# Clearing the other semaphores under the last store, with one wait that takes the store's semaphore back to zero

## Chip, cores, metric

One core of one Trainium2 chip. The metric is the device time of one execution in microseconds (us), taken as the median of several executions. A *span* is the time from the first to the last instruction of the program in the trace. A *semaphore* is a counter that engines and transfers change and that engines wait for. "Landing" is the last of the sixteen increments by which a transfer reports to its semaphore. A *drain* (DRAIN in the lists) is the instruction with which an engine lets its own work end: in the kernel before, those of ScalarE and VectorE ended 34 and 48 ns behind the last work of their engine. Engines are named as in the views: SP issues the transfers here, DVE is VectorE, ACT ScalarE, POOL (Pool) GpSimd, PE TensorE; a q behind the name (POOLq) marks the engine's sequencer, with its waits, drains and semaphore instructions.

## The reference

```python
batch, seq, dim = 32, 512, 1024
x = np.random.randn(batch, seq, dim).astype(np.float32)      # 67.1 MB
return np.sum(x, axis=-1).astype(np.float32)                 # 16384 sums
```

## The kernel before

The body loads seven tiles of 128 x 16 rows and pieces of an eighth, sums them on VectorE (part of the last ones on ScalarE), and stores 16384 sums with two transfers. The one that ends last is issued by SP:

```python
        hold(store(nc.scalar, 0, last), two, "its packets come behind those of the loads")
        halves(whole[:, :1], part)
        halves(sums[:, j : j + 1], whole)
        store(nc.sync, last, last + 1)          # 8 KB, reports to semaphore 105
```

Behind the body the framework puts an end: all engines meet at a barrier (each reports to a "gather" semaphore, Pool passes it and raises a "release" semaphore), Pool clears the semaphores 99 to 108 that the program used, and all meet again. The kernel rewrites this end. SP no longer waits for the store; Pool's clear does, and Pool passes the second gather ahead of it:

```python
def wait_for_the_store_at_the_clear(nc):
    end = nc.main_func.blocks[-1]
    insts = list(end.instructions)
    ...                                   # take the wait for the last store off SP's drain
    clear = next(k for k, i in enumerate(insts)
                 if i.engine == mybir.EngineType.Pool and isinstance(i, mybir.InstISA))
    insts[clear] = copy.replace(
        insts[clear], sync_info=mybir.SyncInfo(on_wait=[wait], on_update=[])
    )
    at = next(k for k in range(clear + 1, len(insts))
              if insts[k].engine == mybir.EngineType.Pool
              and isinstance(insts[k], mybir.InstEventSemaphore))
    met = insts.pop(at)                   # Pool's side of the second gather
    insts.insert(clear, met)
    end.instructions = insts
```

Pool's last instructions are thus: gather, clear of ten semaphores that waits for 105, drain, release.

## Time and profile before

| | kernel before |
|---|---|
| time, first three runs | 161.58, 161.58, 161.99 us |
| span of the profiled run (161.66 us) | 159.88 us |
| last vector sum ends | 158.10 us |
| last store issued / landed | 158.127 / 159.563 us |
| Pool's last instruction ends / span ends | 159.789 / 159.877 us |

Lines of the page and of the list of the last instructions are in the prediction. One view more is needed later: the chain of work that ended last, in order of time (start us, us, what). Lines from its middle and its end, kernel before:

```profile
66.94 40.78 DMA t<-in_x_dram
107.72 0.02 issue
107.75 17.23 DVE sums L141
...
126.33 31.29 DMA t<-in_x_dram
157.62 0.07 issue
157.69 0.40 DVE t L155
158.09 0.01 DVEq L253
```

A line "DMA" is the wait for one load, from issue to landing. Such waits take up most of the chain, and it stops with the last sum at 158.1 us. What follows is no work to the profile, yet it takes 1.78 us to the end of the span. All numbers below that are finer than the views print are the trace's own time stamps.

### The profile page before, as it was taken

The numbers are of one execution on the slowest core, as the hardware profiler recorded it, in microseconds if no ns is written. First come the engines' busy times: TensorE is split into PE (matmuls) and PEld (weight loads), VectorE is DVE, ScalarE is ACT, GpSimd is POOL, SyncE is SP. The second block draws the span as 40 slices with busy tenths as digits, with TensorE's granted clock in tenths as the row PEclk, the third lists the DMA queues.
The fourth block names the chain that finished last, engine by engine and source line by source line (L and its number), as shares of the span: only waits on it lengthen the run. The fifth ranks groups of instructions, "written<-read, shape, count | busy, mean of one in ns | idle before, by whom it ended". The sixth has DMA issues, their size and how long they took to land.

```text
span 159.9 us, 132 instructions
## 1 busy us (share of the span) xinstructions
DVE 120.6 (75%) x40; ACT 12.0 (8%) x21; POOL 0.2 (0%) x4
## 2 busy tenths in 40 slices
DVE  0029600499985999779995899949999499994955
ACT  3000000000000000000000000000000000003993
POOL 0000000000000000000000000000000000000000
DMA  8899899799699699699699699799898996996994
GB/s 308 380 492 525 361 426 525 328 459 525 295 492 525 262 525 525 262 525 525 262 525 508 279 525 476 312 525 410 377 525 361 426 525 262 525 525 289 400 384 124
DMA packets 2784, 67.18 MB, mean 420 GB/s; under 512 B 1248, under 2 KB 1376, under 8 KB 1504
## 3 DMA queue, kind: packets, MB, share of 16 engines
q1 hardware_dynamic: 1872, 67.12, 97.7%
q10 hardware_dynamic: 912, 0.06, 0.4%
HBM read 67.11 MB, written 0.07 MB: 420 GB/s over the span
## 4 chain that ended last, share of the span: by engine, by line
DMA 71%; DVE 27%; SPq 1%; issue 0%; DVEq 0%
DMA t<-in_x_dram 71%; DVE sums L141 26%; SPq L180 0%; SPq L222 0%; DVE t L155 0%; DVEq L253 0%
## 5 line engine op out<-in xcount | busy, mean ns | idle before, releaser
L141 DVE TENSOR_REDUCE sums<-t 128x16 f32<-128x16384 f32 (+1 forms) x7 | 110.9, 15848 | 33.4 <-DMA t<-in_x_dram 33.4
L168 ACT ACTIVATE unread<-t 128x1024 f32<-128x1024 f32 x10 | 10.1, 1013 | 144.7 <-DMA t<-in_x_dram 144.7
L155 DVE CUSTOM_DVE_ANT_0 t<-t 128x512 f32<-128x512 f32 (+2 forms) x16 | 9.6, 654 | 4.1 <-DMA t<-in_x_dram 4.0
L168 ACT ACTIVATION_READ_ACCUMULATOR unread<-t 128x1 f32 x10 | 1.9, 188 | 0.0
L168 ACT ACT_TABLE_LOAD x1 | 1.3, 1283 | 0.8 <-PEq L242 0.8
L155 DVE DVE_READ_ACCUMULATOR2_ANT sums<- 128x1 f32 x15 | 1.2, 81 | 0.0
L242 POOL MEMSET const-bfloat16-1.0<- 128x1 bf16 x1 | 0.1, 102 | 0.0
L242 POOL MEMSET const-uint8-127<- 128x1 uint8 x1 | 0.1, 102 | 0.0
L242 POOL MEMSET const-float32-1.0<- 128x1 f32 x1 | 0.1, 99 | 0.0
L242 POOL MEMSET const-float32-0.0<- 128x1 f32 x1 | 0.1, 98 | 0.2 <-issue 0.2
L155 DVE DVE_READ_ACCUMULATOR2_ANT t<- 128x1 f32 x1 | 0.1, 83 | 0.0
L220 DVE MEMSET t<- 128x1 f32 x1 | 0.1, 59 | 0.0
## 6 DMA issues: line engine op xcount, KB each, us to landing
t<-in_x_dram SPq DMA_DIRECT2D x1, 3584.0 KB, 11.0
t<-in_x_dram SPq DMA_DIRECT2D x1, 3072.0 KB, 28.9
t<-in_x_dram SPq DMA_DIRECT2D x1, 1024.0 KB, 31.0
t<-in_x_dram SPq DMA_DIRECT2D x1, 280.0 KB, 31.2
t<-in_x_dram SPq DMA_DIRECT2D x1, 232.0 KB, 31.3
t<-in_x_dram SPq DMA_DIRECT2D x7, 40.8
out_dram<-sums ACTq DMA_DIRECT2D x1, 56.0 KB, 2.1
out_dram<-sums SPq DMA_DIRECT2D x1, 8.0 KB, 1.4
```

Of the source, the lines that this page charges most:

```text
L141: return nc.vector.tensor_reduce(out=dst, in_=src, axis=mybir.AxisListType.X, op=mybir.AluOpType.add)
L155: return nc.vector.tensor_tensor_reduce(out=src[:, :n], in0=src[:, :n], in1=src[:, n:], scale=1.0, scalar=0.0, op0=mybir.AluOpType.add, op ...
L168: nc.scalar.activation(out=unread[:, :n], in_=src, func=mybir.ActivationFunctionType.Copy, accum_out=dst,)
L220: nc.vector.memset(whole[:, width + 1 :], 0.0)
L242: nc = _bacc.Bacc("TRN2", target_bir_lowering=False, num_devices=1)
```

## The change

The intent: of the ten semaphores only 105 must wait for the store. So the other nine are cleared while the store is under way, and so is Pool's drain passed. Behind the landing stands one semaphore instruction that waits for 105 and subtracts the value again, then the release.

```diff
-    insts[clear] = copy.replace(
-        insts[clear], sync_info=mybir.SyncInfo(on_wait=[wait], on_update=[])
-    )
 ...
-    met = insts.pop(at)
-    insts.insert(clear, met)
+    both = insts[clear]
+    lo, hi = both.ant_dict["range_first"], both.ant_dict["range_last"]
+    def ranged(first, last):
+        instr = list(both.instr)
+        instr[13:15] = first, last
+        ant_dict = dict(both.ant_dict, range_first=first, range_last=last)
+        return copy.replace(
+            both, name=nc.get_next_instruction_name(), instr=instr, ant_dict=ant_dict
+        )
+    ...                                   # met, drain: Pool's side of the second gather and
+                                          # its drain, which stood behind the clear
+    (gather,) = met.sync_info.on_update
+    back = copy.replace(
+        gather, id=wait.id, ant_name=wait.ant_name, update_value=wait.wait_value
+    )
+    taken = copy.replace(
+        met,
+        name=nc.get_next_instruction_name(),
+        sync_info=mybir.SyncInfo(on_wait=[wait], on_update=[back]),
+    )
+    insts = [i for i in insts if i is not met and i is not drain]
+    insts[clear : clear + 1] = [
+        met,
+        ranged(lo, wait.id - 1),
+        ranged(wait.id + 1, hi),
+        drain,
+        taken,
+    ]
     end.instructions = insts
```

More of the change, by code (lines that the diff above doesn't have):

```diff
@@ L82, in wait_for_the_store_at_the_clear @@
     )
-    info = insts[clear].sync_info
-    assert info is None or not (info.on_wait or info.on_update)
-    insts[clear] = copy.replace(
-        insts[clear], sync_info=mybir.SyncInfo(on_wait=[wait], on_update=[])
-    )
-    at = next(
-        k
-        for k in range(clear + 1, len(insts))
-        if insts[k].engine == mybir.EngineType.Pool and isinstance(insts[k], mybir.InstEventSemaphore)
-    )
-    assert insts[at].sync_info.on_wait and "gather" in insts[at].sync_info.on_wait[0].ant_name
-    met = insts.pop(at)
-    insts.insert(clear, met)
+    both = insts[clear]
+    assert both.op_name == "EVENT_SEMAPHORE_RANGE_CLEAR"
+    assert both.sync_info is None or not (both.sync_info.on_wait or both.sync_info.on_update)
+    lo, hi = both.ant_dict["range_first"], both.ant_dict["range_last"]
+    assert (both.instr[13], both.instr[14]) == (lo, hi) and lo < wait.id < hi
+    def ranged(first, last):
[5 more added lines that the diff above has]
+        )
+    met, drain = [
+        insts[k]
+        for k in range(clear + 1, len(insts))
+        if insts[k].engine == mybir.EngineType.Pool
+        and isinstance(insts[k], (mybir.InstEventSemaphore, mybir.InstDrain))
+    ][:2][::-1]
+    assert isinstance(met, mybir.InstEventSemaphore) and isinstance(drain, mybir.InstDrain)
+    (gather,) = met.sync_info.on_update
+    back = copy.replace(
+        gather, id=wait.id, ant_name=wait.ant_name, update_value=wait.wait_value
+    )
+    taken = copy.replace(
+        met,
+        name=nc.get_next_instruction_name(),
+        sync_info=mybir.SyncInfo(on_wait=[wait], on_update=[back]),
+    )
+    insts = [i for i in insts if i is not met and i is not drain]
[6 more added lines that the diff above has]
+    ]
     end.instructions = insts
```

## The prediction

> **What bounds the kernel now.** I read the page first: the busy shares, the slices and the chain that ended last.
>
> ```profile
> span 159.9 us, 132 instructions
> DVE 120.6 (75%) x40; ACT 12.0 (8%) x21; POOL 0.2 (0%) x4
> DMA  8899899799699699699699699799898996996994
> DMA 71%; DVE 27%; SPq 1%; issue 0%; DVEq 0%
> ```
>
> The first line is the length of the program on the core; the third is the DMA engines' busy share in 40 slices of 4 us. The kernel reads 67.11 MB and its body is a stream of loads with vector sums behind them: loads and sums make up 98% of the chain. The change touches none of it. It concerns what stands after the last sum, where the chain of the page stops (at 158.1 us), because the page counts waits, drains and semaphore instructions as no work. So I went on to the views of the end: the list of line L253 (the end of the program) and the stores.
>
> ```profile
> L253 POOLq EVENT_SEMAPHORE_RANGE_CLEAR  x1: 93/93/93, 159.6 to 159.6; - x1
> L253 POOLq DRAIN  x1: 34/34/34, 159.7 to 159.7; - x1
> L253 POOLq EVENT_SEMAPHORE  x1: 17/17/17, 159.8 to 159.8; - x1
> L253 SPq EVENT_SEMAPHORE  x1: 17/17/17, 159.8 to 159.8; - x1
> L253 ACTq EVENT_SEMAPHORE  x1: 17/17/17, 159.8 to 159.8; - x1
> L253 DVEq EVENT_SEMAPHORE  x1: 21/21/21, 159.8 to 159.8; - x1
> L253 PEldq EVENT_SEMAPHORE  x1: 51/51/51, 159.8 to 159.8; - x1
> ...
> out_dram<-sums SPq DMA_DIRECT2D x1, 8.0 KB, 1.4
> ```
>
> Columns of the first seven: engine, operation, count, shortest/median/longest duration in ns, start in us. They are the last seven instructions, from 159.58 us on; the eighth line is the last store, 8 KB, 1.4 us from issue to landing. The views print starts to a tenth of a us. This change needs nanoseconds, so I read the trace's own time stamps (us from the span's start):
>
> - 158.093: the last vector sum ends; 158.127 to 158.475: SP issues the last store, on semaphore 105.
> - 158.877 to 158.894: Pool passes the first gather barrier; 158.955 to 158.972: it releases the others; 159.036 to 159.106: its drain.
> - 159.180: the fourth engine reports to the second gather; 159.204 to 159.221: Pool passes it. From here Pool stands still for 366 ns.
> - 159.386 to 159.563: the sixteen increments of semaphore 105 arrive, 12 ns apart. The last is the landing of the store.
> - 159.587 to 159.680: range clear of semaphores 99 to 108, which waits for 105 to reach 32. The ten land between 159.608 and 159.652 in bunches of four, four and two, about 20 ns apart.
> - 159.709 to 159.743: Pool's drain. 159.772 to 159.789: Pool releases the other four. 159.814 to 159.877: they leave; PE's 51 ns end the span.
>
> So what bounds the tail is the store's landing, and after it a row of 314 ns (159.877 - 159.563) in series on Pool: 24 to wake, 93 clear, 29 gap, 34 drain, 29 gap, 17 release, and 88 until PE is out.
>
> **What the Trainium skill says.** Perfetto Trace Analysis, section "Sequencer-only Instruction (DRAIN, etc)": the profiler's start is the moment at which all semaphores are satisfied, and neither the wait nor the propagation of an update is in the duration. The trace agrees: durations are 7 to 93 ns, and what costs as much are the gaps (24, 29, 61 ns), so I count start to start. DMA: Bandwidth & Descriptors, section "Why a DMA increments its semaphore by 16 and not by 1": each engine that a store uses adds 1 after its own data, and only the full count means that all has landed. The trace shows exactly sixteen increments of 105, over 177 ns. It follows that 105 must not be cleared before 159.563, while the rest of the range has no such bar. Runtime: NRT & Kernel Launch, section "The ~15µs preamble/postamble breakdown": after the kernel come barriers and a reset of the semaphores. No view here names these stages; the profiled run took 161.66 us against a span of 159.88, so 1.78 us of the metric lie outside the span and the change does not touch them.
>
> **The change, part by part.** Pool's end was: gather, [wait 105] clear 99-108, drain, release. It becomes: gather, clear 99-104, clear 106-108, drain, [wait 105, subtract 32], release. The other four engines and all of the body stay as they are.
>
> What moves ahead of the landing, timed from 159.204 where the gather is passed (unchanged): A semaphore instruction that also updates is followed by the next one 78 ns after its own start: Pool's 158.877 to 158.955, and the same pair at the beginning of the program, 0.582 to 0.660. So the first clear starts at 159.282. The old clear shows 21 ns before its first write, bunches 20 ns apart, and 28 ns after the last write: 93 for three bunches. Six semaphores are two bunches, about 73 ns; three are one, about 51 ns (estimates from this one instruction). With the 29 ns gap seen behind the old clear: first clear 159.282 to 159.355, second 159.384 to 159.435, drain (34) 159.464 to 159.498, ready for the wait at about 159.527. The landing comes at 159.563 and is noticed at 159.587 (24 ns, as the old clear was, and as the gather's 159.180 to 159.204). There are some 60 ns of slack to the noticed landing. If each clear costs a full 93 ns whatever its range, the sum is 159.282 + 93 + 29 + 93 + 29 + 34 + 29 = 159.589, which is late by 2 ns. So this part is free, or nearly, in this trace.
>
> What stays behind the landing: the wait-and-subtract starts at 159.587; the release starts 78 ns later, at 159.665. The pair is of the very form of the two gather/release pairs above, only with another semaphore and 32 in place of 4. Before, the release started at 159.772: 93 + 29 + 34 + 29 = 185 ns after the wake. The gain is 185 - 78 = 107 ns. From the release to the end of PE's exit are 105 ns, unchanged (159.772 to 159.877). The span becomes 159.77.
>
> What it adds: two instructions on Pool (one clear more, and the wait-and-subtract), both counted above. The sum: 161.58 - 0.107 = 161.47 us, or 0.07% less. I choose the median of before as base, which two of the three runs hit.
>
> **The rivals.** First, *the early work isn't hidden after all*: the landing must come after the drain is done. For: the slack is only 60 ns, and the sixteen increments of 105 arrive (159.386 on) just while the clears write to the neighbours of 105. If a clear is held back, or if the gap behind it is 61 ns rather than 29, Pool is late. Against: even with two clears of 93 ns and every gap at 61, the wait starts at 159.282 + 93 + 61 + 93 + 61 + 34 + 61 = 159.685, 98 ns later than the landing is noticed, and the gain is 107 - 98 = 9 ns: 161.57. A dear case costs nothing, it only eats the gain. Second, *the subtraction is dearer than on the barrier's semaphores*, as 105 has just been written to by sixteen DMA engines. The gather's 96 is also written by four engines just before and shows no such cost; I put it at 0 to 50 ns: 161.47 to 161.52. Third, *the end of the span moves and the time doesn't*, because the 1.78 us outside it wait for something else, an instruction fetch for instance. In this trace the next write to a semaphore comes 235 ns after the span's end, and nothing shows what it waits for: 161.58. Fourth, *the runs scatter by more than the gain*: the three runs of before lie 0.41 us apart and the profiled one gives 161.66. That is four times the gain, and it comes from the stream of loads, where one delayed transfer moves all of the rest. For a median from another chip I allow 0.3 us either way.
>
> **Range and chances.** All mechanisms together lie between 161.47 and 161.58, so scatter sets the width: 161.15 to 161.8. For 2% it would take 3.2 us; the whole tail from the last sum to the end of the span is 1.78 us (158.093 to 159.877). Faster by 2% can't come from here, and slower by 2% would need a disturbed run. I give 0.99 to the same, and the rest to accidents.
>
> **What would show it.** In the trace of the changed kernel: two range clears on Pool, both ended before the last increment of 105, the first shorter than 93 ns and the second shorter still; a Pool drain ended before it too; one more Pool semaphore instruction of 17 ns that starts 24 ns after the landing; the release 78 ns behind that; and 207 ns, not 314, from landing to the end of the span. These differences within one trace hold even if the span itself moves by several tenths through its loads. It is wrong if a clear or the drain still stands after the landing, if the step from the wait to the release is much over 78 ns, or if the landing itself comes later after its issue than 1.44 us (158.127 to 159.563), which would mean that the clears disturb it. The time is wrong in its mechanism if landing to end shrinks by 107 ns and interleaved timed runs of both kernels show no difference near 0.1 us; a difference of several tenths either way I would read as the loads' scatter.

## The result and the profile after

The changed kernel: 161.89 us median of six runs (161.45 to 162.05), the kernel before 161.60 us median of six (161.55 to 161.99), ratio 1.0009 with a 95% interval of 0.9993 to 1.0026: the same. A ratio here is the mean time of one kernel's fast runs over that of the other's of the same rounds, so not quite the ratio of the medians. Executions over 1.5% slower than the fastest of the same kernel are left out of the means.

So no gain shows, rather the opposite by 0.09%. The profile of the changed kernel (a run of 161.81 us) has to say which part of it is the change. Its end, as the list of the end's instructions (columns as in the prediction), first the stretch from the gather to the landing, then the one behind the landing:

```profile
L279 POOLq EVENT_SEMAPHORE_RANGE_CLEAR  x2: 46/58/71, 159.6 to 159.7; - x2
L279 POOLq DRAIN  x1: 34/34/34, 159.7 to 159.7; - x1
```

```profile
L279 POOLq EVENT_SEMAPHORE  x2: 17/17/17, 159.9 to 159.9; - x2
L279 SPq EVENT_SEMAPHORE  x1: 17/17/17, 160.0 to 160.0; - x1
L279 ACTq EVENT_SEMAPHORE  x1: 17/17/17, 160.0 to 160.0; - x1
L279 DVEq EVENT_SEMAPHORE  x1: 21/21/21, 160.0 to 160.0; - x1
L279 PEldq EVENT_SEMAPHORE  x1: 51/51/51, 160.0 to 160.0; - x1
```

There are two clears of 71 and 46 ns where one of 93 stood, and they and the drain have left the stretch behind the landing. Only two semaphore instructions of 17 ns and the four exits remain there. The time stamps: gather 159.473, clears 159.554 to 159.625 and 159.651 to 159.697, drain to 159.760, landing 159.827, wait-and-subtract 159.851, release 159.930, end of the span 160.034. From landing to end are 207 ns, before they were 314.

Yet the span is 160.03 us, longer by 0.16. The same chain as above, changed kernel:

```profile
67.05 40.99 DMA t<-in_x_dram
108.04 0.02 issue
108.07 17.23 DVE sums L167
...
126.68 31.22 DMA t<-in_x_dram
157.90 0.06 issue
157.96 0.40 DVE t L181
158.36 0.01 DVEq L279
```

The sums take 17.23 us as before; the load of 40.78 us took 40.99, and the last sum ends at 158.37 us in place of 158.10. So the body came 0.27 us later, and the end is 0.11 us shorter; together 0.16 more. Is the later body chance, or did the change cause it? And does the shorter end reach the time at all? These are the questions for the experiments.

### The profile page after: what moved, and what is told of

It reads as the page before. It is cut to its first block, busy times and chain, and to the rows that moved or that the text cites. A ratio compares the mean times of both kernels' runs of the same rounds, so it can differ in the third digit from the quotient of the medians.

```text
span 160.0 us, 134 instructions
## 1 busy us (share of the span) xinstructions
DVE 120.6 (75%) x40; ACT 11.9 (7%) x21; POOL 0.2 (0%) x4
## 4 chain that ended last, share of the span: by engine, by line
DMA 71%; DVE 27%; SPq 1%; issue 0%; DVEq 0%
DMA t<-in_x_dram 71%; DVE sums L167 26%; SPq L206 0%; SPq L248 0%; DVE t L181 0%; DVEq L279 0%
```

## The experiments

Twelve kernels ran. For each full-size kernel one profile gives a row of this table; all are in us. "Landing to time" is the time of the profiled execution minus its landing, so the body and its scatter are out of it. Tail kinds: see the sections below.

| profile of | last sum ends | landing to Pool's end | landing to span's end | time | time - Pool's end | time - span's end | landing to time |
|---|---|---|---|---|---|---|---|
| before | 158.10 | 0.226 | 0.314 | 161.66 | 1.871 | 1.783 | 2.097 |
| changed | 158.37 | 0.120 | 0.207 | 161.81 | 1.863 | 1.776 | 1.983 |
| e1, changed again | 158.08 | 0.118 | 0.207 | 161.53 | 1.870 | 1.781 | 1.988 |
| e2, before again | 158.76 | 0.226 | 0.314 | 162.31 | 1.866 | 1.778 | 2.092 |
| e3, dear tail | 157.95 | 1.097 | 1.185 | 162.38 | 1.874 | 1.786 | 2.971 |
| e4, wait last | 158.07 | 0.081 | 0.081 | 161.48 | 1.872 | 1.872 | 1.953 |
| e8, shortest end | 158.50 | 0.040 | 0.040 | 161.88 | 1.883 | 1.883 | 1.923 |
| e9, drain alone | 158.39 | 0.162 | 0.250 | 161.88 | 1.871 | 1.783 | 2.033 |
| e10, clears alone | 158.07 | 0.185 | 0.272 | 161.58 | 1.869 | 1.782 | 2.054 |
| e11, ScalarE tail | 158.00 | 0.119 | 0.475 | 161.44 | 1.865 | 1.509 | 1.984 |
| e12, before again | 158.00 | 0.225 | 0.313 | 161.55 | 1.864 | 1.776 | 2.089 |

My theory after the result: the end is 107 ns shorter in every execution, and the loads scatter by several tenths of a us whichever end follows. Rival A: the change disturbs the loads. Rival B: the time outside the span swallows what happens at the span's end. Runs 1 to 4 shared a chip and their runs of the kernel before (161.57 us median of eleven); so did 5 to 8. Of 9 to 11 only the profile was taken.

### e1: the changed kernel again

Edit: a comment.

> The changed kernel, unchanged but for a comment, in more timed runs. My theory (the tail is 107 ns shorter, and the stream of loads scatters by several tenths of a us whichever tail follows): landing of the last store to end of span 207 ns again (205 to 209), the last vector sum ends anywhere from 157.9 to 158.6 us, times from 161.4 to 162.1 us, and a ratio to the kernel before between 0.998 and 1.002. Rival A (the change disturbs the loads, so that they end later): ratio over 1.001 again, and the last sum ends near 158.36 us, as in the first trace of the changed kernel, not near 158.09.

Measured: 161.59 us median of six (161.38 to 162.27), ratio 1.0002 (0.9984 to 1.0021). One run lies above the range that I gave (162.27) and one just below it (161.38). The last sum ends at 158.08 us, earlier than in the first profile of the kernel before; landing to end is 207 ns. Rival A, which had the last sum near 158.36 again, falls in its simple form.

### e2: the kernel before against itself

Edit: a comment in the kernel before.

> The kernel before against itself, the same program under a new name. My theory: here too the times of one kernel lie in two clusters or a band some 0.5 us wide (161.5 to 162.1), and the ratio to itself strays from 1 by up to 0.002, so that 1.0009 of the changed kernel is what no change at all can give. Landing to end of span 314 ns. Rival A: the kernel before stays close to 161.6 us (all but one of six runs did), ratio within 0.0005 of 1.

Measured: 161.89 us median of five (161.68 to 162.31) against 161.57 for the very same program, ratio 1.0012 (0.9997 to 1.0026). Two names of one program differ by more than the changed kernel differed from it. The chain of this run, from the same places as above:

```profile
66.97 41.49 DMA t<-in_x_dram
108.46 0.02 issue
108.48 17.23 DVE sums L141
...
158.35 0.40 DVE t L155
158.75 0.01 DVEq L253
```

The load of 40.78 us took 41.49 here, with nothing changed. The starts of the seven big sums show how it comes: 19.31 to 19.36 us lie between one and the next in the first profile of the kernel before; here three of the six steps are 19.67, 19.65 and 19.45; in the first profile of the changed kernel 19.49, 19.42 and 19.38 stand out. A few tiles come late, now these, now those, and little of it is made up: the seventh big sum starts 0.75 us later than in the first profile, the last sum ends 0.66 us later.

### e3: a known cost where the change saves

```diff
         drain,
         taken,
-    ]
+    ] + [copy.replace(drain, name=nc.get_next_instruction_name()) for _ in range(16)]
```

> The changed kernel with sixteen more drains on Pool between the wait-and-subtract and the release: a known cost at the place where the change saves. My theory: each drain costs 34 + 29 = 63 ns, sixteen 1.01 us, landing to end of span 207 + 1010 = 1.22 us, and the time rises by the same 1.0 us over the changed kernel of the same call: about 162.6 to 162.9 us, ratio about 1.006 to the kernel before. Rival B (the time outside the span swallows what happens at the end of the span): span longer by 1.0 us but the time by under 0.5 us.

The sixteen drains stand in the list of the end, with the one ahead of the landing:

```profile
L279 POOLq DRAIN  x17: 34/34/34, 159.3 to 160.4; - x17
```

Measured: landing to end 1.185 us, 0.98 more than with the changed end (a drain and its gap took 61 ns, not 63). The time: 162.54 us median of five against 161.59 for e1, 0.95 more; ratio to before 1.0055 (1.0041 to 1.0069). The median is 0.06 below what I gave. Free of the body, landing to time is 2.971 against 1.988 us of e1: 0.983, all of it. Rival B falls: a cost at this place reaches the time in full.

### e4: the wait behind the release

```diff
-        drain,
-        taken,
-    ]
+        drain,
+    ]
+    k = next(
+        k
+        for k in range(insts.index(drain) + 1, len(insts))
+        if insts[k].engine == mybir.EngineType.Pool
+        and isinstance(insts[k], mybir.InstEventSemaphore)
+    )
+    insts.insert(k + 1, taken)
```

> The changed kernel with the wait-and-subtract moved behind the release: the other four engines leave before the store has landed, and Pool alone waits. My theory: landing to end of span 24 + 17 = 41 ns in place of 207, another 166 ns saved; the time 161.3 to 161.9 us, since the loads scatter by more; ratio about 0.998, interval wide enough to touch 1. Rival B: the ends of the other engines or something behind the span set the time, and nothing more is gained in the time, though landing to end is 41 ns. Another rival: the four waits that leave early delay the noticing of the landing, and landing to end is 80 ns or more.

The last two semaphore instructions of Pool and PE's exit, in the list of the end:

```profile
L285 POOLq EVENT_SEMAPHORE  x2: 17/17/17, 159.5 to 159.6; - x2
L285 PEldq EVENT_SEMAPHORE  x1: 51/51/51, 159.5 to 159.5; - x1
```

Measured: landing to end 81 ns, not 41, the number of the last rival named. The release ended 15 ns ahead of the landing, and the wait started 79 ns behind the release (64 behind the landing), where 24 ns behind the landing would have done. That the four engines that leave caused it, as this rival has it, isn't shown; in e8 the clear behind the release started after 63 ns although they left then too, and a gather in e7 and e8 was late by as much with no engine leaving (see the list at the end). Timed: 161.54 us median of six (161.41 to 162.07), ratio 0.9996 (0.9981 to 1.0010), where I gave about 0.998. The surprise is in the table: the end of the span moved 126 ns nearer to the landing than in e1, but the time moved only 35 ns (1.988 to 1.953), and time minus the span's end grew from 1.78 to 1.87 us. What stayed the same, in all six profiles by then, is the time minus the end of *Pool's* last instruction. Hence theory C: the time follows Pool's end, and the exits of the other engines behind it, PE's 51 ns among them, cost nothing.

### e5, e6, e7: three ends behind a short body

```diff
-        rows(t, 0, FIRST, j, 0)
+        nc.vector.memset(sums, 0.0)
+        rows(t, 0, 1, j, 0)
...
-                load = rows(t, 0, BIG, g * BIG, 0)
+                load = rows(t, 0, 1, g * BIG, 0)
             else:
-                rows(t, 0, BIG, g * BIG, 7, pairs=True)
+                rows(t, 0, 2, g * BIG, 1, pairs=True)
...
-        rows(t, FIRST, 6, j + FIRST, 2, pairs=True)
+        rows(t, FIRST, 2, j + FIRST, 1, pairs=True)
```

The result is wrong on purpose. e5 has the end of the kernel before, e6 the changed one, e7 the end of e8 below.

> The end of the kernel before, behind a body cut short: each load brings one or two of its 16 rows, the other sums are set to zero (wrong result on purpose; the same fourteen transfers, semaphores and end). With some 6 MB in place of 67 the stream that scatters is short. My theory: landing of the last store to end of span 314 ns; five or six times within 0.15 us of each other; the time itself some 18 to 25 us.

> The end of the changed kernel behind the same short body. My theory: landing to end 207 ns, and in the medians of this run and the one of the old end with the short body the difference shows: 0.11 us less (0.07 to 0.15). Rival B (nothing of the tail reaches the time): medians within 0.03 us of each other though the tails differ by 107 ns.

> Short body; on Pool the drain before the second gather, then gather, release, the two clears, and the wait-and-subtract as its last instruction. In the runs so far the time lies 1.86 to 1.87 us behind the end of Pool's last instruction, in all six traces, also where the wait came last (there the time lay 1.87 us behind the span's end, otherwise 1.78). New theory C: the time follows Pool's last end. Here Pool is ready before the landing and ends 41 ns behind it, not 120 as in the changed kernel: 0.08 us less than the changed end with the short body, 0.19 less than the old end. Rival: the wait is again passed late (landing to Pool's end 80 ns), 0.04 us less than the changed end.

Measured, as a timing: a miss. The medians of the fast runs are 29.16 us (five runs, 29.06 to 29.20), 29.06 (three, 28.91 to 29.08; the slow ones took 29.71 to 30.71) and 29.32 (four, 29.24 to 29.43). The program was longer than I had estimated. e6 lies 0.10 us below e5, as expected, but e7, with the shortest end, lies 0.16 us above e5 where 0.19 less was expected: in its profile the last sum ends 0.21 us later than in that of e5. So these medians decide nothing. As traces they confirm the steps: landing to end 314, 207 and 41 ns. Landing to time is 2.093, 1.994 and 1.914 us, and time minus Pool's end 1.868, 1.875 and 1.873 us.

### e8: the shortest end behind the full body

```diff
     insts[clear : clear + 1] = [
+        drain,
         met,
+        release,
         ranged(lo, wait.id - 1),
         ranged(wait.id + 1, hi),
-        drain,
         taken,
     ]
```

(The release is taken out of its old place.) The drain is passed ahead of the gather, and the release ahead of the clears, so Pool is ready before the landing.

> The same end as in the run before (drain, gather, release, clears, wait-and-subtract last) behind the full body. Landing to Pool's end, which is the end of the span, 41 ns; time minus end of Pool 1.87 us. The fastest of its runs at about 161.3 us, against 161.52 for the kernel before and 161.38 for the changed one; the ratio to before 0.998 to 1.000, not clear of the scatter of the loads.

Measured: landing to Pool's end 40 ns as expected, time minus Pool's end 1.883 us, 13 ns more than I gave. Landing to time is 1.923 us, 0.17 less than for the kernel before. The timed runs don't show it: 161.88 us median of five (161.40 to 162.12) against 161.63, ratio 1.0006 (0.9990 to 1.0022); fastest and ratio both lie above what I gave (161.3, and 0.998 to 1.000). This version has the shortest end of all; that it beats either kernel in time isn't shown.

### e9, e10: the parts of the change alone

In e9 the kernel before gets the drain moved, in e10 the changed kernel gets the drain put back:

```diff
+    drain = insts.pop(drain)              # e9: Pool's drain behind the clear
-    insts.insert(clear, met)
+    insts[clear:clear] = [met, drain]
```

```diff
-        drain,
         taken,
+        drain,
     ]
```

> The kernel before with one part of the change: Pool's drain stands before the clear that waits for the store, and the clear of all ten semaphores stays behind the landing. My theory by its steps: release starts 24 + 93 + 29 = 146 ns behind the landing in place of 209, landing to end of span 251 ns: 63 of the 107 ns come from the drain. Rival: behind the clear an EVENT_SEMAPHORE needs a longer gap than a drain does (61 ns), release at 178.

> The changed kernel with the drain put back behind the landing: clears ahead, wait-and-subtract, drain, release. My theory by its steps: 24 + 17 + 64 + 34 + 29 = 168 ns from landing to release (the gap of 64 is the one seen between a release and a drain), 41 ns less than the kernel before, landing to end 273 ns. With the run that moves the drain alone the parts are 63 and 41, together 104 of the 107 seen for both. Rival: the clears give most of the gain because they are the longest single instruction (93 ns), landing to end under 250.

Measured: landing to end 250 and 272 ns, within 1 ns of both. In the list of the end, e9 first, then e10:

```profile
L259 POOLq DRAIN  x1: 34/34/34, 159.6 to 159.6; - x1
L259 POOLq EVENT_SEMAPHORE_RANGE_CLEAR  x1: 93/93/93, 159.9 to 159.9; - x1
```

```profile
L279 POOLq EVENT_SEMAPHORE_RANGE_CLEAR  x2: 46/58/71, 159.3 to 159.4; - x2
L279 POOLq EVENT_SEMAPHORE  x2: 17/17/17, 159.6 to 159.7; - x2
L279 POOLq DRAIN  x1: 34/34/34, 159.6 to 159.6; - x1
```

In e9 the drain stands ahead of the landing (159.847) and the whole clear behind it; in e10 the clears stand ahead of it (159.526) and the drain behind. The drain gives 64 ns, the clears 42: 106 of the 107 for both. The clear is the longest instruction of the end, but the drain's move is worth more, since what takes the clear's place behind the landing, 17 ns and a gap of 61 to 64, costs most of what is won.

### e11: ScalarE ends last

```diff
+    left = max(
+        k
+        for k, i in enumerate(insts)
+        if i.engine == mybir.EngineType.Activation and isinstance(i, mybir.InstEventSemaphore)
+    )
+    insts[left + 1 : left + 1] = [
+        copy.replace(drain, name=nc.get_next_instruction_name(), engine=mybir.EngineType.Activation)
+        for _ in range(8)
+    ]
     end.instructions = insts
```

> The changed kernel with eight drains on ScalarE behind its last instruction, so that ScalarE and not PE ends the span, some 0.3 to 0.5 us later than Pool ends. Theory C (the time follows Pool's last end): time minus Pool's end stays at 1.86 to 1.88 us, time minus the span's end falls to 1.4 to 1.5. Rival (the time follows the end of the span): time minus the span's end stays at 1.78 us and time minus Pool's end grows to 2.2 or more.

The end of this kernel, in the list of its instructions:

```profile
L288 ACTq DRAIN  x8: 8/8/8, 159.7 to 159.9; - x8
L288 POOLq EVENT_SEMAPHORE  x2: 17/17/17, 159.5 to 159.6; - x2
...
L288 PEldq EVENT_SEMAPHORE  x1: 51/51/51, 159.6 to 159.6; - x1
```

ScalarE's eight drains end at 159.931 us, 356 ns behind Pool (159.575) and 268 behind PE. The time minus Pool's end is 1.865 us, within the 1.863 to 1.883 of all profiles; the time minus the span's end falls to 1.509, a little above what I gave. Theory C holds: a span longer by 0.27 us cost nothing. The traces say the same without the time: in all fourteen the next write to semaphore 105 (behind its own clear or subtraction) comes 901 to 904 ns behind Pool's end. Semaphore 2, which no instruction of the program names, is next written 323 and 357 ns behind Pool's end in the kernel before, and a third time at 562. In e11 the second of these writes came at 463; in e8, where the other engines left 0.19 us and more ahead of Pool, the first two came at 42 and 76. The third came at 561 to 563 in all fourteen. How long another engine may stay behind before the time notices was not tried.

### e12: the kernel before against itself, once more

Edit: the one of e2.

> The kernel before against itself once more, alone in its turn. If a copy under a new name is slower than the base by its place or its turn (a bias of the comparison), the ratio is again 1.0005 to 1.002 and under half of its times lie below 161.7 us, where the base has most of its own. If the ratio of the first such run (1.0012) was the chance of five runs, this one lies between 0.9985 and 1.0005. Landing to end of span 314 ns, time minus Pool's end 1.86 to 1.88 us either way.

Measured: 161.55 us median of six (161.51 to 161.66) against 161.78 of eleven for the base, ratio 0.9983 (0.9965 to 1.0002). The sign is turned around. So the 1.0012 of e2 was no fixed bias against a second name, though the ratio lies a little outside the range that I gave for chance. The same program against itself gives 1.0012 and 0.9983; the changed kernel's 1.0009 and 1.0002 lie between them.

## Why the prediction was right

*The work ahead of the landing is free*: right. From the gather's start to the first clear were 81 ns (78 predicted), the clears 71 and 46 (73 and 51), the gaps 26 and 29 (29). The drain ended 67 ns ahead of the landing (65 by the estimate). The landing itself came 1.431 us after its issue, 1.436 before: the clears of the neighbours did not disturb it.

*What stays behind it*: right. Wake 24 ns, wait to release 79 (78 predicted), landing to end 207 (207). e9 and e10 split the saving of 107 into 64 and 42, by the same durations and gaps.

*The gain reaches the time*: right, and shown free of the body, though not by the timed runs. Landing to time averages 2.093 us over the four profiles with the old end (before, e2, e5, e12) and 1.987 over the four with the changed one (changed, e1, e6, e11): 0.106 us less, with at most 11 ns between the four of a kind. The third rival, a time that doesn't move, falls. By the prediction's own sign the mechanism would have been wrong, since landing to end shrank by 107 ns and interleaved runs of both kernels showed no gain near 0.1 us (ratios 1.0009 and 1.0002). That sign was badly chosen: runs that differ by 0.4 us and more without any change can't show it.

*1.78 us lie outside the span, and the change does not touch them*: right for this change only. The constant is 1.86 to 1.88 us behind Pool's end. It looked like 1.78 behind the span's end, because PE leaves 87 to 89 ns after Pool in both kernels.

*The scatter exceeds the gain*: right, and it was mis-sized. That the class is "the same" followed from the size of the tail alone and says nothing for the mechanism. I took the time to be 161.58 - 0.107, as if the body would repeat the best cluster of the runs of before. The six runs of the changed kernel had a median of 161.89 us, 0.09 above my range; 161.60 times the ratio of 1.0009, 161.75, is inside. The term that failed is that base, not the 0.107: the body of single profiles of the full-size kernels ended anywhere from 157.95 to 158.76 us, 0.81 us of scatter, nearly eight times the gain. Even the fastest runs only hint at the gain: 161.38 us of twelve for the changed kernel, 161.51 of 51 for the one before, over several chips.

Two readings of the trace in the prediction are a little off, without effect on its sum. 158.093 is the end of the last vector operation; its accumulator is read until 158.099. And not all durations of the end are 7 to 93 ns: the drains of ScalarE and VectorE that wait for their engines' last work took 649 and 371 ns.

What stays open: why single tiles come up to 0.3 us late. It happens to the unchanged program too, and up to the second gather (159.473 us in the changed kernel) Pool runs the same instructions in both kernels, while the late tiles come well before. That the change makes it a little more or less likely isn't excluded by a dozen runs.

## What to carry to other kernels

When a change moves a tenth of a microsecond behind a body that scatters by more, don't ask the medians: measure from an event that both kernels share (here the last store's landing) to the end *and* to the time of the same execution, and run the old kernel against itself before you believe a ratio near 1. Put behind a late event only what truly depends on it, and count the gaps behind semaphore instructions along with their durations: moving a 34 ns drain gave more than splitting a 93 ns clear. And find out which engine's end the time follows before you shorten the span; here it was Pool's: in e4 PE ended 8 ns ahead of Pool in place of 87 behind it, and the time kept its distance from Pool's end alone.

## What the Trainium skill lacked or had wrong

- Perfetto Trace Analysis, section "Sequencer-only Instruction (DRAIN, etc)": it rightly says that waits and propagation are outside the reported duration, but gives no sizes. Here: 23 to 24 ns from the last increment to the start of the instruction with which Pool waits for it; and where Pool's next instruction has no wait, 61 to 64 ns to it from the end of an updating semaphore instruction, 26 to 30 ns from that of a clear or a drain. Where the next instruction has a wait and its semaphore fills only 14 or 15 ns behind the one ahead, it was later: 79 ns behind the release in e4, 44 ns behind the drain in e7 and e8, some 15 ns more than without a wait; why isn't shown.
- No page has the cost of a range clear on Pool: 93 ns for ten semaphores, 71 for six, 46 to 48 for three, with writes in bunches of four some 20 ns apart.
- Runtime: NRT & Kernel Launch, section "The ~15µs preamble/postamble breakdown": it lists what follows the kernel, not what it is counted from. In all profiles here the time lies 1.86 to 1.88 us behind Pool's last instruction, also where ScalarE ended 356 ns after Pool.
- DMA: Bandwidth & Descriptors, section "Why a DMA increments its semaphore by 16 and not by 1": sixteen increments, as the traces show. It does not say how they are spaced: at the last store they came about 12 ns apart, 0.18 us from first to last.
